# Sums, turns and products set in another order at the first items and at the end of column one

## The chip, the cores and the metric

The kernel runs on one core of one Trainium2 chip. The metric is the time of one execution on the device in microseconds (us), as the median of several runs. Three runs of the kernel before took 1510.43, 1511.97 and 1513.06 us.

## The reference

```
a, b: 4096 x 4096, float32; bias: 4096, float32
reference(a, b, bias) = tanh(a @ b + bias)
```

The output is 4096 x 4096 in float32. The kernel multiplies in fp16 and sums in fp32.

## The kernel before, in words

**Blocks.** The 4096 rows of a are 16 pairs of 2 x 128 rows; the 4096 columns of b are four column groups of 1024, called columns 0 to 3. For one pair and one column group the result has four blocks of 128 x 512. They are made with seven products instead of eight (a Strassen scheme in Winograd's form). The left operands are the four quarters a11, a12, a21, a22 of the pair's rows, turned so that the contraction lies on the partitions (128 x 2048 in fp16), and sums of them: s2 = a21 - a22, s5 = a12 - a11, s1 = a22 - a11, s6 = s2 + s1, s7 = s1 - s5. The right operands are b11 and b22 and the sums d1, d3, d4, e6, e7 of b's quarters, which stay in SBUF for a whole column. The products are m2 (s2, b11), m5 (s5, b22), m3 (a11, d3), m1 (s1, d1), m4 (a22, d4), m6 (s6, e6) and m7 (s7, e7). Each is 16 matmuls of 128 x 128 by 128 x 512 into one PSUM bank.

**Read-outs.** After a product, `after` (for the first three items `lead_after`) emits the steps that read its bank. After m2 VectorE adds the bias to bank z into bank d and subtracts it into s (first items: the bias minus z into bank c); after m5 it writes c = z - s; after m1 it writes cs - z; after m7 it writes o = ds - z. m3, m4 and m6 are read by ScalarE. m5, m1 and m7 accumulate in z, so each waits until the one before it has been read; m3 accumulates in c.

**Items and slots.** The unit of work is an item, a pair (or half the contraction of two pairs) in one column, numbered 0 to 60. Items 0 to 12 are column 0 and 13 to 28 column 1. Seven slots belong to each item: item n has the slots from 7n on, its products stand at fixed positions from there (`PRODUCTS`: m2 at 0, m5 at 2, m3 at 4, m1 at 5, m4 at 6, m6 at 8, m7 at 10), so m6 and m7 of an item lie among the products of the next. For items 0 to 2 (`LEAD` = 3) `FIRST` gives another assignment: m4, m2, m3, m1, m5, m6, m7. At each slot the work put down for it by `at_slot` is emitted first, in the order of registration, and then the product with its read-outs. Every engine runs its own instructions in the order in which they were emitted, so this order, written by hand, is the schedule.

**Natural items.** Items 0 to 12 and 26 to 28 load a from HBM as float32, cast by the DMA to fp16, with `load_nat` (lines 228, 237, 245) on POOL's queue; r = 1 brings the rows of a21 and a22, r = 0 those of a11 and a12, u = 0 and 1 the two halves of each. `turn` then lets VectorE transpose them (line 265), two halves for each quarter. `prepare` puts the turns and sums on slots. Turned quarters that later items use again are stored to DRAM by `keep` on SP's queue; other items fetch them from there by `fetch`.

**Column one's long stretch.** Items 17 to 24 run in pairs through `four`, which applies the scheme a second time (matmuls 256 wide). For it some right operands give up room: quarters of b11 and e6 and one quarter (T3) of d3, d4, b22 and e7 are held in DRAM and brought back at its end. `give_back`, called as `step(k)` from the last call of `four`, emits what the table `BACK` gives for step k: `bring_block` and `move` for the operands, `fetch` for the quarters a21 and a12 of item 25 (guests), `load_nat` for item 26. `move` uses POOL's queue at steps below 12 and SP's from there on. Behind this stretch come items 25 to 28, the end of column one; 27 and 28 each take half the contraction of two pairs and lead over to column two.

**The main loop** goes over the slots and, in each, over `PRODUCTS`; with the positions before, at most one product falls on a slot.

All VectorE sums have line 151 (`tt`), products outside `four` line 473, those inside 765 and 829.

Of the kernel before, what the change touches and what calls it, by code (L numbers as in the profile page):

```python
# [35 lines left out]
PRODUCTS = {  # L36
    0: ("m2", "s2", "b11"),
    2: ("m5", "s5", "b22"),
    4: ("m3", "a11", "d3"),
    5: ("m1", "s1", "d1"),  # L40
    6: ("m4", "a22", "d4"),
    8: ("m6", "s6", "e6"),
    10: ("m7", "s7", "e7"),
}
SLOTS = 7

LEAD = 3
FIRST = {0: 6, 2: 0, 4: 4, 5: 5, 6: 2, 8: 8, 10: 10}  # L50

LAST = (ds(0, 384), ds(384, 128))
# [38 lines left out]

BACK = {
    1: {
        ("e6", 0): 6, ("e6", 1): 7, ("m7", "t3"): 7, ("b11", 0): 10, ("b11", 1): 10, ("b11", 2): 10, ("b11", 3): 10,
        ("m5", "t3"): 10, ("m3", "t3"): 10,
        ("guest", "a21"): 8, ("guest", "a12"): 10, ("nat", 1): 11, ("m4", "t3"): 11,
    },
# [23 lines left out]
def kernel(  # L121
# [61 lines left out]
    partner, begins, ends_with, firsts = {}, {}, {}, {}  # L183
# [10 lines left out]
    twos = {*partner, *second}  # L194
    fours = {n for c in FOURS for n in range(begins[c], ends_with[c])}
    guests = {(ends_with[1], "a12"), (ends_with[1], "a21")}

    def beginning(n):
        return begins.get(items[n][0], len(items))

    def again(n):
        return items[n][3]

# [12 lines left out]

    nat, aset = {}, {}

    def load_nat(n, r):


        c, pairs, part, _ = items[n]
        for u in range(2):
            if n < LEAD:
                tl = wide.tile([P, 4, KQ // 2], fp16, name="nat", tag="wide")
                for q in (0, 2, 1, 3):
                    src = a[ds((2 * pairs[0] + r) * P, P), ds(q * KQ + u * KQ // 2, KQ // 2)]
                    nc.gpsimd.dma_start(  # L228
                        out=tl[ds(q * QP, QP), :, :],
                        in_=src.rearrange("(mb p) k -> p mb k", p=QP),  # L230
                    )
            elif part is None:
                pool, tag = (quads, ("a21", "a12")[u]) if n - 2 in fours and not r else (wide, "wide")
                tl = pool.tile([P, 2, KQ], fp16, name="nat", tag=tag)
                for q in (0, 2, 1, 3):
                    src = a[ds((2 * pairs[0] + r) * P + u * 2 * QP, 2 * QP), ds(q * KQ, KQ)]
                    nc.gpsimd.dma_start(  # L237
                        out=tl[ds(q * QP, QP), :, :],
                        in_=src.rearrange("(mb p) k -> p mb k", p=QP),
                    )  # L240
            else:
                tl = wide.tile([P, 4, KQ // 2], fp16, name="nat", tag="wide")
                for q in (0, 2, 1, 3):
                    src = a[ds((2 * pairs[u] + r) * P, P), ds(q * KQ + part * KQ // 2, KQ // 2)]
                    nc.gpsimd.dma_start(
                        out=tl[ds(q * QP, QP), :, :],
                        in_=src.rearrange("(mb p) k -> p mb k", p=QP),
                    )
            nat[n, r, u] = tl
# [55 lines left out]
    turns = [0]  # L305
# [547 lines left out]
    def give_back(c, step):  # L853
        for (name, part), at in BACK[c].items():
            if at == step:
                if name == "nat":
                    load_nat(ends_with[c] + 1, part)
                elif name == "guest":
                    fetch(ends_with[c], part)
                elif name in TWO:  # L860
                    move(name, c, False, part, queue=nc.gpsimd if step < 12 else nc.sync)
                elif name in ("b12", "b21"):
                    load_raw(name, c + 1, part, nc.sync)
                else:
                    bring_block(name, part)
# [441 lines left out]
    def prepare(n):  # L1307

        s0 = SLOTS * (n - 1)
        part = items[n][2]  # L1310
        if again(n):
            at_slot(s0, lambda: aset[n].update((i, aset[n - 2][i]) for i in QUADS))
        elif natural(n):
            loads = {0: (-5, -4), 1: (4, 5), 2: (6, 7)}.get(n, (s0 - 7, s0 - 4))
            for r in (1, 0):
                at_slot(loads[1 - r], load_nat, n, r)
                if n == 1 and r:
                    at_slot(loads[0], store_ends, "A")
            turns = {
# [4 lines left out]
            }.get(n, [(i, (s0 + x, s0 + y)) for i, (x, y) in {  # L1324
                "a22": (0, 0), "a21": (2, 2), "a11": (3, 4), "a12": (5, 5)
            }.items()])
            if n - 2 in fours:
                turns = [("a22", (3, 3)), ("a21", (4, 4)), ("a11", (5, 5)), ("a12", (6, 6))]
                turns = [(i, (s0 + x, s0 + y)) for i, (x, y) in turns]
            for name, at in turns:  # L1330
                at_slot(at[0], turn, n, name, 0)
            for name, at in turns:
                at_slot(at[1], turn, n, name, 1)
                if n == 0 and name == "a22":
                    at_slot(-1, asum, n, "s2", 0)
                if name in ("a11", "a22") and not stays(n):
                    at_slot({0: {'a22': -1, 'a11': 5}, 1: {'a22': 12, 'a11': 15}, 2: {'a22': 17, 'a11': 18}}.get(n, {}).get(name, at[1]), keep, n, name)
        else:
            behind = n - 2 in partner
            for name, at in (  # L1340
                ("a22", 1 if behind else 0), ("a21", 1),
                ("a11", -1 if n in second else 0 if behind else 2), ("a12", 4),
            ):
                if part == 1 and n - 2 in fours and name != "a12":
                    continue
                if name == "a12" and n - 2 not in twos and n > LEAD + 1 and n - 2 not in fours:
                    early_fetch.add(n)
                elif name != "a12" or n - 2 not in twos:
                    at_slot(s0 + at, fetch, n, name)
        late = stays(n)  # L1350
        end_ = n == len(items) - 1
        sums_at = {"s2": 4, "s5": 6, "s1": 9}
        sums_at["s6"] = 12 if late else 13 if end_ else 10
        sums_at["s7"] = 15 if late else 12 if end_ else 13
        if n == 0:
            at_slot(-1, asum, n, "s2", 1)
            at_slot(-1, keep, n, "a21")
            sums_at = {"s1": 10, "s5": 11, "s6": 12, "s7": 14}
        elif n == 1:
            sums_at = {"s2": 6, "s1": 9, "s5": 9, "s6": 13, "s7": 15}  # L1360
        elif n == 2:
            sums_at = {"s2": 6, "s1": 8, "s5": 9, "s6": 12, "s7": 14}
        elif n == 3:
            sums_at["s2"] = 3
        elif n - 2 in partner:
            sums_at["s2"] = 3
        if natural(n) and n - 2 in fours:
            sums_at["s2"], sums_at["s5"] = 5, 7
        if n - 2 in twos and n not in twos and part is None:
            sums_at["s5"] = 8  # L1370
        for name, at in sums_at.items():
            at_slot(s0 + at, asum, n, name)
            if natural(n) and name in ("s2", "s5") and not stays(n):
                at_slot(s0 + at, keep, n, "a21" if name == "s2" else "a12")
        if natural(n) and stays(n):
            for at, name in zip(LATER[part], ("a22", "a21", "a11", "a12")):
                at_slot(SLOTS * (n + 2) + at, keep, n, name)
        if n < LEAD:
            at_slot(s0 + 11, lead_add, n)
            if n:  # L1380
                at_slot(s0 + 4, lead_bias, n)
# [255 lines left out]
    for c in range(1, NC):  # L1637
        n = next(n for n in range(len(items)) if items[n][0] == c)
# [33 lines left out]
    for n in partner:  # L1672
        s0 = SLOTS * n
# [15 lines left out]
    for slot in range(1 - len(ORDER), SLOTS * len(items)):  # L1689
# [11 lines left out]
        elif slot == 3:  # L1701
            last_visit(0)
            last_visit(1)
        for pos, p in PRODUCTS.items():
            n, r = divmod(slot - pos, SLOTS)
            if r == 0 and n >= 0 and n not in fours:
                if n < LEAD:
                    product(n, *PRODUCTS[FIRST[pos]])
                elif p[0] not in ("m3", "m4") or n not in twos:
                    product(n, *p)  # L1710
        for group in groups.get(slot, ()):
            twice_four(*group)
# [30 lines left out]
```

## Time and profile before

| | |
|---|---|
| median of three runs | 1511.97 us (1510.43 to 1513.06) |
| the profiled execution's own time | 1510.32 us |
| its span, first to last instruction | 1508.6 us |
| mean granted TensorE clock | 0.999 |
| TensorE busy | 1495.9 us (99%) |
| VectorE busy | 1214.4 us (80%) |
| ScalarE busy | 402.9 us (27%) |
| POOL busy | 528.4 us (35%) |

The profile is one execution, and its times count from the first instruction. PE is TensorE, PEld its weight load, DVE is VectorE, ACT is ScalarE, SP issues DMAs only. A row of a timeline has its start, its duration, engine, line, operation, the tiles written and read, the shape and the number of instructions merged into it; a bracket has the idle time of the engine before the row and what ended it. Matmuls overlap, and their ends are modelled, so a row of 16 is drawn a little longer than the distance to the next. Rows of the windows' view have, for each engine, busy time and instructions, and at the end the granted clock, the DMA engines' busy share and GB/s. In the view of waits the three figures are the sum in us, the number and the longest.

### The profile page before, as it was taken

The page shows a single profiled execution, that of the slowest core. Times are in us where ns is not written, and L with a number is a line of the kernel's source. Part 1 is how long each engine was busy: PE and PEld are TensorE (multiplying, and loading weights), DVE is VectorE, ACT ScalarE, POOL GpSimd, SP SyncE. Part 2 cuts the span into 40 slices and gives each one's busy share as a digit, 9 for nine tenths or more (in the row PEclk, how much of TensorE's full clock was granted, in tenths as well). Part 3 has the DMA queues.
Part 4 walks back from the last instruction along what each step waited for, and adds up shares of the span by engine and source line. Part 5 has one row for each costly group of instructions (what it writes and reads, how often), then busy time and mean ns, then how long its engine had stood idle before and what let it go on. Part 6 is the DMA issues. An engine that isn't in the chain of part 4 may idle for free.

```text
span 1508.6 us, 24955 instructions
## 1 busy us (share of the span) xinstructions
PE 1495.9 (99%) x9461; PEld 925.3 (61%) x9461; DVE 1214.4 (80%) x1718; ACT 402.9 (27%) x909; POOL 528.4 (35%) x925
## 2 busy tenths in 40 slices
PE   9999999999999999998999999999999999999999
PEld 4444444444445788863444578888744458888887
DVE  6788977778787888967788788888758869888888
ACT  4431111111222233321123223333212222333332
POOL 8765454434523111255660321111434121111112
PEclk9999999999999999999999999999999999999999
DMA  9999999999999799899999988998899687888895
GB/s 183 178 243 265 294 265 258 226 220 178 183 345 308 259 324 344 309 317 255 186 265 324 276 267 317 335 342 303 307 304 225 201 277 274 303 312 305 321 345 190
DMA packets 209020, 412.47 MB, mean 273 GB/s; under 512 B 26114, under 2 KB 100354, under 8 KB 208900
## 3 DMA queue, kind: packets, MB, share of 16 engines
q0 software_dynamic: 124992, 220.00, 59.6%
q1 hardware_dynamic: 83236, 190.49, 35.6%
q8 instruction: 74, 1.21, 0.3%
q10 hardware_dynamic: 672, 0.39, 0.1%
q14 instruction: 46, 0.38, 0.1%
HBM read 351.80 MB, written 138.41 MB: 325 GB/s over the span
## 4 chain that ended last, share of the span: by engine, by line
PE 90%; DMA 6%; POOL 1%; issue 1%; DVE 1%; ACT 0%; POOLq 0%; DVEq 0%
PE ps L473 41%; PE ps L765 37%; PE ps L829 7%; PE ps L1419 5%; DMA nat<-in_a_dram 4%; DMA d<-away_m_t 1%; DMA out_dram<-o 1%; DMA e<-form_m 0%; DVE a L265 0%; DMA side<-in_b_dram 0%; POOL nat L228 0%; POOL nat L237 0%; POOL out_dram L1557 0%; ACT o L1552 0%; DVE a L151 0%
## 5 line engine op out<-in xcount | busy, mean ns | idle before, releaser
L473 PEld LDWEIGHTS <-a 128*128 128x128 f16 x2592 | 253.9, 98 | 312.2 <-issue 9.9
L765 PEld LDWEIGHTS <-h 128*128 128x128 f16 x2944 | 288.0, 98 | 35.8
L701 POOL DMA_DIRECT2D form<-form_m x196 | 103.9, 530 | 538.0 <-PE ps L765 484.8
L765 PEld LDWEIGHTS <-a 128*128 128x128 f16 x2208 | 216.0, 98 | 34.0 <-issue 0.9
L473 PE MATMUL ps<-b,a 128*128 128x512 f16 x868 | 200.0, 381 | 4.2 <-DVE s L151 4.2
L473 PE MATMUL ps<-d,a 128*128 128x512 f16 x800 | 180.8, 379 | 2.2 <-DVE ps L151 2.2
L265 DVE STREAM_TRANSPOSE a<-nat 128x1024 f16<-128x1024 f16 (+3 forms) x178 | 155.9, 918 | 23.0 <-PE ps L473 13.1
L473 PE MATMUL ps<-e,a 128*128 128x512 f16 x700 | 159.2, 379 | 0.0
L151 DVE TENSOR_TENSOR a<-a,a 128x2048 f16<-128x2048 f16 (+1 forms) x123 | 148.0, 1203 | 0.2
L765 PE MATMUL ps<-form,h 128*128 128x256 f16 x1136 | 144.8, 273 | 0.0
L375 POOL DMA_DIRECT2D b<-in_b_dram x208 | 112.0, 546 | 87.7 <-PE ps L473 32.0
L151 DVE TENSOR_TENSOR h<-a,h 128x1024 f16<-128x1024 f16 x184 | 124.8, 685 | 16.6 <-PE ps L765 16.5
L473 PEld LDWEIGHTS <-s 128*128 128x128 f16 x688 | 67.3, 98 | 79.9
L473 PE MATMUL ps<-d,s 128*128 128x512 f16 x496 | 112.1, 379 | 0.0
L765 PE MATMUL ps<-form,a 128*128 128x256 f16 x896 | 111.5, 273 | 0.2
L829 PE MATMUL ps<-d,a 128*128 128x512 f16 x480 | 108.2, 379 | 0.0
L237 POOL DMA_DIRECT2D nat<-in_a_dram x144 | 76.4, 541 | 76.6 <-DMA nat<-in_a_dram 35.0
L851 ACT CAST ps<-zeros 128x256 f32<-128x256 f16 x192 | 68.8, 380 | 128.6 <-DVE s L151 69.0
L829 PEld LDWEIGHTS <-a 128*128 128x128 f16 x608 | 59.5, 98 | 65.9
L151 DVE TENSOR_TENSOR ds<-ds,ps 128x512 f32<-128x512 f32 (+1 forms) x126 | 83.3, 672 | 9.2 <-PE ps L829 8.3
L151 DVE TENSOR_TENSOR ps<-ps,x 128x256 f32<-128x256 f32 x96 | 41.2, 429 | 47.3 <-PE ps L765 37.6
L498 ACT ACTIVATE o<-ps 128x512 f32<-128x512 f32 x78 | 46.9, 601 | 117.4 <-issue 69.8
(167 smaller groups left out, 1971.3 us busy)
## 6 DMA issues: line engine op xcount, KB each, us to landing
form<-form_m POOLq DMA_DIRECT2D x196, 512.0 KB, 7.3
a<-scratch SPq DMA_DIRECT2D x148, 512.0 KB, 7.5
out_dram<-o SPq DMA_DIRECT2D x186, 256.0 KB, 6.1
nat<-in_a_dram POOLq DMA_DIRECT2D x256, 128.0 KB, 6.9
scratch<-a SPq DMA_DIRECT2D x48, 512.0 KB, 7.2
b<-in_b_dram POOLq DMA_DIRECT2D x176, 128.0 KB, 5.6
form_m<-stage POOLq DMA_DIRECT2D x18, 512.0 KB, 6.0
scratch<-a SPq DMA_DIRECT2D x32, 256.0 KB, 7.7
```

What stands on the lines that cost most here:

```text
L151: nc.vector.tensor_tensor(out=out_, in0=in0, in1=in1, op=op)
L237: nc.gpsimd.dma_start(out=tl[ds(q * QP, QP), :, :], in_=src.rearrange("(mb p) k -> p mb k", p=QP),)
L265: nc.vector.transpose(dst[:, ds(b0 * tb, n * tb), :].rearrange("P (b t) (mb p) -> P mb b t p", t=tb, p=QP), src[:, :, ds(b0, n), :].rearra ...
L375: nc.gpsimd.dma_start(out=dst[ds(q * QP, QP), ds(t, nt)], in_=src)
L473: nc.tensor.matmul(st[where], at, bt, start=(what == "m2" or n < LEAD and what == "m1") and i == 0, stop=i == len(ts_) - 1, skip_group_che ...
L498: nc.scalar.activation(o, src, TANH)
L701: nc.gpsimd.dma_start(out=rights[what, name], in_=forms[what, name])
L765: nc.tensor.matmul(to, at, bt, start=False, stop=t == TP - 1, skip_group_check=True)
L829: nc.tensor.matmul(to[:, half], at[:, t // TB, t % TB], bop[right, t // TB][:, t % TB, half], start=anew and t == 0, stop=t == T - 1, skip ...
L851: nc.scalar.copy(bank(n, 0, where)[:, HALF[half]], zeros)
L1419: nc.tensor.matmul(mb[m % 4, j], aq[m, kt // T][:, kt % T, :], right(kt, j), start=fresh and kt == k0, stop=stop and kt == k1 - 1, skip_gr ...
```

## The change

It moves work among slots and queues; the arithmetic stays.

- Item 1: s1 and s5 go from slot 9 to 10, item 2: s5 from 16 to 17, so behind the read-out of their own item's m2. Item 4: the turns of a22 go from slot 21 to 22, behind the read-outs of item 3's m2.
- Item 26: the second halves of a11 and a12 are turned at slot 183 instead of 180 and 181, and s5 goes from 182 to 183; m2 of item 26 is at 182. Item 27: a22 is turned at 183 and 184 instead of 182. The two keeps of a11 and of s5 go with them.
- m7 of item 25 is put at position 9 instead of 10, which is slot 184, where it is emitted ahead of m5 of item 26. m4 of item 26 is put at position 3 instead of 6, ahead of m3.
- The end of the long stretch: the T3 quarter of d3 goes from step 10 to step 11, behind the loads of item 26's r = 1 rows; that of d4 from step 11 to step 14, which is on SP's queue. The fetch of the guest a12 is emitted ahead of b11 (another queue).

```diff
+BEHIND = {"m7": 9}, {"m4": 3}
...
 BACK = {
     1: {
-        ("e6", 0): 6, ("e6", 1): 7, ("m7", "t3"): 7, ("b11", 0): 10, ("b11", 1): 10, ("b11", 2): 10, ("b11", 3): 10,
-        ("m5", "t3"): 10, ("m3", "t3"): 10,
-        ("guest", "a21"): 8, ("guest", "a12"): 10, ("nat", 1): 11, ("m4", "t3"): 11,
+        ("e6", 0): 6, ("e6", 1): 7, ("m7", "t3"): 7, ("guest", "a21"): 8, ("guest", "a12"): 10,
+        ("b11", 0): 10, ("b11", 1): 10, ("b11", 2): 10, ("b11", 3): 10,
+        ("m5", "t3"): 10, ("nat", 0): 11, ("nat", 1): 11, ("m3", "t3"): 11, ("m4", "t3"): 14,
     },
...
+    def order_of(n):
+        if n < LEAD:
+            return [(pos, PRODUCTS[FIRST[pos]]) for pos in PRODUCTS]
+        moved = {ends_with[1]: BEHIND[0], ends_with[1] + 1: BEHIND[1]}.get(n, {})
+        return sorted((moved.get(p[0], pos), p) for pos, p in PRODUCTS.items())
...
-    def load_nat(n, r):
+    def load_nat(n, r, parts=(0, 1)):
         c, pairs, part, _ = items[n]
-        for u in range(2):
+        for u in parts:
...
                 if name == "nat":
-                    load_nat(ends_with[c] + 1, part)
+                    load_nat(ends_with[c] + 1, 1, (part,))
...
+            if n == 4:
+                turns[0] = "a22", (s0 + 1, s0 + 1)
+            if n - 3 in fours and part is not None:
+                turns[0] = "a22", (s0 + 1, s0 + 2)
             if n - 2 in fours:
-                turns = [("a22", (3, 3)), ("a21", (4, 4)), ("a11", (5, 5)), ("a12", (6, 6))]
+                turns = [("a22", (3, 3)), ("a21", (4, 4)), ("a11", (5, 8)), ("a12", (6, 8))]
...
         elif n == 1:
-            sums_at = {"s2": 6, "s1": 9, "s5": 9, "s6": 13, "s7": 15}
+            sums_at = {"s2": 6, "s1": 10, "s5": 10, "s6": 13, "s7": 15}
         elif n == 2:
-            sums_at = {"s2": 6, "s1": 8, "s5": 9, "s6": 12, "s7": 14}
+            sums_at = {"s2": 6, "s1": 8, "s5": 10, "s6": 12, "s7": 14}
...
         if natural(n) and n - 2 in fours:
-            sums_at["s2"], sums_at["s5"] = 5, 7
+            sums_at["s2"], sums_at["s5"] = 5, 8
...
-        for pos, p in PRODUCTS.items():
-            n, r = divmod(slot - pos, SLOTS)
-            if r == 0 and n >= 0 and n not in fours:
-                if n < LEAD:
-                    product(n, *PRODUCTS[FIRST[pos]])
-                elif p[0] not in ("m3", "m4") or n not in twos:
+        for n in (slot // SLOTS - 1, slot // SLOTS):
+            if n < 0 or n in fours:
+                continue
+            for pos, p in order_of(n):
+                if SLOTS * n + pos == slot and (p[0] not in ("m3", "m4") or n not in twos):
                     product(n, *p)
```

## The prediction

> **What bounds the kernel now.** I read the busy shares first, then the waits of TensorE, its timeline around each wait, and last the timelines of the engines and queues that end those waits.
>
> ```profile
> PE 1495.9 (99%) x9461; PEld 925.3 (61%) x9461; DVE 1214.4 (80%) x1718; ACT 402.9 (27%) x909; POOL 528.4 (35%) x925
> ```
>
> TensorE is busy for 1495.9 of 1508.6 us, so only its own gaps can be won. The view of waits, for TensorE alone, names those inside the kernel:
>
> ```profile
> PE ps L473 <- DVE s L151: 4.2, 2, 3.5
> PE ps L473 <- DVE ps L151: 2.2, 2, 1.8
> PE ps L473 <- DVE a L151: 0.4, 1, 0.4
> ```
>
> Five waits, all on VectorE (DVE). The timeline of TensorE places them; the bracket is the idle time before the row.
>
> ```profile
> 120.51 3.62 PE L473 MATMUL ps<-e,a 128*128 128x512 f16 x16
> 125.94 3.61 PE L473 MATMUL ps<-d,a 128*128 128x512 f16 x16 [1.82 <-DVE ps L151]
> ...
> 150.61 3.61 PE L473 MATMUL ps<-d,a 128*128 128x512 f16 x16 [0.34 <-DVE ps L151]
> ...
> 168.73 3.61 PE L473 MATMUL ps<-b,a 128*128 128x512 f16 x16 [0.69 <-DVE s L151]
> ...
> 699.75 1.04 PE L473 MATMUL ps<-side,a 128*128 128x512 f16 x4 [0.42 <-DVE a L151]
> ...
> 710.33 5.30 PE L473 MATMUL ps<-b,a 128*128 128x512 f16 x16 [3.50 <-DVE s L151]
> ```
>
> From the chain of waits, two long pieces with no gap follow the two groups, and one transfer precedes them:
>
> ```profile
> 139.17 8.35 DMA nat<-in_a_dram
> ...
> 168.73 293.69 PE ps L473 x1360
> ...
> 710.33 126.17 PE ps L473 x576
> ```
>
> A product of 16 matmuls thus takes 16 x 293.69 / 1360 = 3.455 us. The product of 120.51 should be followed at 123.97 and was followed at 125.94: 1.97 lost, 0.15 more than its bracket (the drawn end of a matmul overlaps the next start). So the losses are 1.97, 0.50, 0.85, 0.58 and 3.66. The row at 710.33 lasts 5.30 instead of 3.62, 1.68 more, and the stretch shows why:
>
> ```profile
> 709.90:713.40 3.50, 3.07 (x9) 1.18 (x9) 3.50 (x6) 0.00 (x0) 1.33 (x3) 0.62 1.16 256
> ```
>
> The granted clock (third figure from the end) was 0.62 after the idle time of 3.50; after the one of 1.82 the product took its usual 3.61. [...]
>
> All the losses together are 1.97 + 0.50 + 0.85 + 0.58 + 3.66 + 1.68 = 9.24 us, the most that the change can win.
>
> **Part one, the first items (3.3 us of loss).** VectorE's timeline ahead of the three waits:
>
> ```profile
> 120.67 2.37 DVE L265 STREAM_TRANSPOSE a<-nat 128x1024 f16<-128x1024 f16 x2 [2.22 <-DMA nat<-in_a_dram]
> 122.97 1.18 DVE L151 TENSOR_TENSOR s<-a,a 128x2048 f16<-128x2048 f16 x1
> 124.07 1.21 DVE L151 TENSOR_TENSOR a<-a,a 128x2048 f16<-128x2048 f16 x1
> 125.20 0.69 DVE L151 TENSOR_TENSOR ps<-bias_bc,ps 128x512 f32<-128x512 f32 x1
> ...
> 147.60 1.25 DVE L265 STREAM_TRANSPOSE a<-nat 128x1024 f16<-128x1024 f16 x1 [1.74 <-DMA nat<-in_a_dram]
> 148.77 1.18 DVE L151 TENSOR_TENSOR a<-a,a 128x2048 f16<-128x2048 f16 x1
> 149.87 0.69 DVE L151 TENSOR_TENSOR ps<-bias_bc,ps 128x512 f32<-128x512 f32 x1
> ...
> 165.15 2.36 DVE L265 STREAM_TRANSPOSE a<-nat 128x1024 f16<-128x1024 f16 x2
> ```
>
> Item 1: its s1 and s5 (122.97, 124.07) stand ahead of m2's read-out (125.20), for which m3 waits. Put behind, the read-out runs at 122.97 and ends at 123.66, before m3 is due at 123.97: the 1.97 go. The sums then run where they end no later than now plus one read-out, about 125.9; m1, the first user of s1, is due at 127.4 and m5 at 130.9. Nothing else on VectorE moves.
>
> Item 2: only s5 (148.77) moves. The turn at 147.60 stays ahead of the read-out, and it waits for a transfer issued at 139.17 that lands 8.35 later, at 147.5. TensorE being early does not hurry that transfer. The read-out runs 148.77 to 149.46, so m3 starts at 149.50 instead of 150.61. It is due at 150.11 - 1.97 = 148.14, so 1.36 is lost anew: of the first 2.47 us, 1.11 remains.
>
> Item 3: m5 is due five products after 149.50, at 166.78. The two turns of 165.15 (item 4's a22) go one slot back, behind m2's two read-outs, which then run 165.15 to 166.5 and are in time. So 168.73 becomes 166.78. Item 4's a22 is then turned by 168.9; its first user, the sum s2, stands two slots after the turn's new one.
>
> Part one gives 1.95 us. From there the gapless piece of 293.69 only moves; VectorE has no new work.
>
> **Part two, behind column one (5.9 us of loss).** Times are those of before, without the shift. VectorE and TensorE:
>
> ```profile
> 697.28 1.30 DVE L265 STREAM_TRANSPOSE a<-nat 128x256 f16<-128x256 f16 x2 [1.74 <-DMA nat<-in_a_dram]
> 698.51 1.18 DVE L151 TENSOR_TENSOR a<-a,a 128x2048 f16<-128x2048 f16 x1
> ...
> 704.88 1.24 DVE L265 STREAM_TRANSPOSE a<-nat 128x1024 f16<-128x1024 f16 x1
> 707.86 1.25 DVE L265 STREAM_TRANSPOSE a<-nat 128x1024 f16<-128x1024 f16 x1 [1.73 <-DMA nat<-in_a_dram]
> ...
> 709.60 0.67 DVE L151 TENSOR_TENSOR s<-ps,bias_bc 128x512 f32<-128x512 f32 x1
> ...
> 711.33 2.48 DVE L265 STREAM_TRANSPOSE a<-nat 128x512 f16<-128x512 f16 x4
> ```
>
> ```profile
> 688.81 3.62 PE L473 MATMUL ps<-d,a 128*128 128x512 f16 x16
> ...
> 729.28 1.03 PE L473 MATMUL ps<-side,a 128*128 128x512 f16 x4
> ```
>
> 688.81 is item 25's m3, and m1 and m4 follow. The second half of item 26's a11 goes behind m2's read-outs, so s2 (698.51) starts near 695.5, when VectorE now begins its wait, and ends at 696.7: m2 of item 26 is on time at 699.17. It ends at 702.6; m6 and now m7 of item 25 fill TensorE to 709.54, when m5 is due. VectorE meanwhile: read-outs to 704.1, the halves of a11 and a12 (1.30, 1.2) to 706.6, s5 (1.2) to 707.8. So m5 waits for nothing, 1.7 to spare: 0.58, 3.66 and 1.68 all go, 5.92 together.
>
> What takes their place must fit: item 27's a22 and a21 (1.24, then s1 with 1.2, 1.25, 2.48), m7's last step and m5's read-out (0.7 each) take VectorE to about 715. m3 right behind m5 would be due at 713.0 and wait 2; with m4 between them it is due at 716.45. At the end m2 of item 27 comes at 723.36 instead of 729.28. Its four read-outs stand behind m1's read-out, two sums (1.2 each) and two turns (2.4), the first two done by 729.9 against m5's 730.3: covered by 0.4, because m4 no longer lies between.
>
> **The T3 transfers.** POOL issues in order:
>
> ```profile
> 672.17 0.75 POOL L627 DMA_DIRECT2D d<-away_m_t  x1 [0.35 <-DMA b<-form_m]
> ...
> 675.51 1.16 POOL L237 DMA_DIRECT2D nat<-in_a_dram  x2 [1.12 <-DMA b<-form_m]
> ...
> 684.06 1.55 POOL L627 DMA_DIRECT2D d<-away_m_t  x2
> ...
> 691.73 0.53 POOL L237 DMA_DIRECT2D nat<-in_a_dram  x1 [0.58 <-DMA d<-away_m_t]
> ```
>
> ```profile
> 672.17 10.04 DMA d<-away_m_t
> ...
> 684.06 6.28 DMA d<-away_m_t
> ```
>
> At 672.17 m3's pair goes out, then eight loads for item 26, then at 684.06 m4's pair. m3's pair now goes behind the eight loads, and m4's to SP's queue, behind the fetch of a11 and ahead of m6's store. m4's is needed at 695.7: free, and the store behind it waits for ScalarE anyway. m3's first half is needed at 688.81, the second four matmuls later at 689.67. Early bound: the loads move up by 675.51 - 672.17 = 3.34, the pair goes out at 680.7, lands after 6.28 at 687.0, the second half about 1 later: no wait. Late bound: it lands as m4's pair does now, at 690.34 and 691.45 (the load of 691.73 waits for it, less an issue gap of 0.28): 1.78. I take 0.8, near the middle, since the same bytes are moved in either order but two issues fewer stand ahead.
>
> [...]
>
> **Sum.** 1.95 + 5.92 - 0.8 = 7.07 us. The profiled execution took 1510.32 (span 1508.6 and 1.7 around it) and would take 1503.2; it lies 1.65 below the median of the runs, 1511.97, from which I forecast 1504.9.
>
> **Rivals.** *T3 late.* POOL holds m3's pair behind loads that each wait for an earlier landing. For: latencies here reach 10.04. Issued at 684.06 with that latency, its halves land at 694.1 and about 694.9: idle 5.2, over the 3.50 that cost clock, so 1.7 more; of 7.87 us, 1 remains, 1511.0. At latency 8 it is 692.9 in the second half, idle 3.2, no clock lost: 4.7 remain, 1507.3. Against: 6.28 for the pair last issued there.
>
> *Slower.* The wait for item 27's tile is not removed but moved: it now stands ahead of m5's read-out, and m3 behind that. The tile landed just before 707.86; the new place is reached at 709.9, and m3 has 1.6 to spare, so it decides from a landing at 711.5 on, 1 us for each us, and 1.7 for the clock once idle passes 3.5. To end 3 us slower than before it must land near 720. For: SP's two keeps, now at one slot, compete. Against: they start after 705, and the landing would have to slip by 12.
>
> *No change:* the DMA paces the first items (the 1.74 and 2.22 waits) and the loads for 26 to 28, so that TensorE, sooner, waits elsewhere for the same landings. Against: behind 168.73 and 710.33 no row of TensorE waits for a DMA or VectorE. Time 1512. In a half form it gives back part one alone: 1506.9.
>
> *More:* no T3 wait and an earlier 147.5: up to 9.24, 1502.7.
>
> **Numbers.** Forecast 0.62 (1504.1 to 1505.9), T3 late 0.15, half form 0.06, more 0.06, no change 0.06, slower 0.05. A difference under 0.2% (3 us) can't be told from none. Faster: forecast, half form, more and most of T3 late, 0.84; same: no change and the rest of it, 0.11; slower 0.05. The range 1502.5 to 1510.0 leaves out the last two cases and the worst T3, and has a little for the spread of the runs.
>
> **What would show it.** Right: no TensorE wait near 124; one of about 0.2 to 1.2 near 149; none near 167; m5 of item 26 without a wait and no stretch with a clock below 1.00 after it; a DMA wait on d before item 25's m3 of 0 to 1.8. Wrong: a wait of m3 over 3 us, a VectorE wait at item 26's m3 or item 27's m5, or a new gap between 200 and 650.

## The result, and the profile after

| | before | after |
|---|---|---|
| median, same chip (6 runs each) | 1510.96 us (1508.90 to 1513.06) | 1503.53 us (1502.12 to 1505.88) |
| the profiled execution's own time | 1510.32 us | 1502.82 us |
| its span | 1508.6 us | 1501.1 us |
| mean granted TensorE clock | 0.999 | 1.0 |

The ratio of the times is 0.9954 (95% interval 0.9940 to 0.9967), a gain of about 7 us. Forecast were 1504.9 us, a gain of 7.07, and a range of 1502.5 to 1510.0. In the diff's new line numbers the sums have line 152, the turns 272, the products 480.

The busy shares of the page after, and the view of waits for TensorE; outside the warm-up only one wait on another engine is left:

```profile
PE 1494.3 (100%) x9461; PEld 925.3 (62%) x9461; DVE 1213.8 (81%) x1718; ACT 403.9 (27%) x909; POOL 527.0 (35%) x923
```

```profile
PE ps L480 <- DVE ps L152: 0.3, 1, 0.3
```

TensorE's timeline after, at the places shown of before (start, duration, operation; the bracket is the idle time ahead):

```profile
120.51 3.62 PE L480 MATMUL ps<-e,a 128*128 128x512 f16 x16
123.96 3.62 PE L480 MATMUL ps<-d,a 128*128 128x512 f16 x16
...
148.60 3.61 PE L480 MATMUL ps<-d,a 128*128 128x512 f16 x16 [0.30 <-DVE ps L152]
...
165.86 3.62 PE L480 MATMUL ps<-b,a 128*128 128x512 f16 x16
...
686.12 3.87 PE L480 MATMUL ps<-d,a 128*128 128x512 f16 x16
...
701.05 6.21 PE L480 MATMUL ps<-e,a 128*128 128x512 f16 x28
707.09 3.62 PE L480 MATMUL ps<-b,a 128*128 128x512 f16 x16
710.54 7.07 PE L480 MATMUL ps<-d,a 128*128 128x512 f16 x32
717.45 3.62 PE L480 MATMUL ps<-d,s 128*128 128x512 f16 x16
720.90 1.03 PE L480 MATMUL ps<-side,a 128*128 128x512 f16 x4
```

Item 1's m3 follows its predecessor after 3.45 us, so its wait is gone. Item 2's m3 starts 0.46 later than a product after 144.68 (start of the one ahead) would let it. Item 3's m5 has no bracket; it stands at 165.86 against 168.73, so TensorE is 2.87 us early. The row of 686.12, item 25's m3, is drawn with 3.87 instead of 3.62: 0.28 us are lost ahead of its first matmul and 0.26 ahead of its fifth, just behind the landings of its T3 pair at 685.98 and 687.20. Behind column one m6 and m7 of item 25 run as one row of 28 matmuls, m5 of item 26 follows at once, m4 and m3 make one row of 32. Item 27's m2 starts at 720.90 against 729.28, 8.38 us early. The clock was never reduced in between, as the windows' view shows (third figure from the end):

```profile
706.90:710.40 3.50, 3.50 (x18) 1.61 (x17) 3.50 (x6) 0.00 (x0) 1.91 (x4) 1.00 1.06 244
```

VectorE's timeline after, at the three places that the change reorders:

```profile
121.76 0.67 DVE L152 TENSOR_TENSOR ps<-bias_bc,ps 128x512 f32<-128x512 f32 x1
122.34 1.20 DVE L152 TENSOR_TENSOR s<-a,a 128x2048 f16<-128x2048 f16 x1
...
146.71 1.25 DVE L272 STREAM_TRANSPOSE a<-nat 128x1024 f16<-128x1024 f16 x1 [2.17 <-DMA nat<-in_a_dram]
147.88 0.67 DVE L152 TENSOR_TENSOR ps<-bias_bc,ps 128x512 f32<-128x512 f32 x1
...
701.00 0.68 DVE L152 TENSOR_TENSOR s<-ps,bias_bc 128x512 f32<-128x512 f32 x1
701.59 2.42 DVE L272 STREAM_TRANSPOSE a<-nat 128x256 f16<-128x256 f16 x3
704.05 1.23 DVE L152 TENSOR_TENSOR a<-a,a 128x2048 f16<-128x2048 f16 x1
...
711.55 0.69 DVE L152 TENSOR_TENSOR ps<-ps,s 128x512 f32<-128x512 f32 x1
```

At 121.76 the read-out is ahead of s1. At 147.88 the read-out still stands behind a turn that waited 2.17 us for its tile. At 701.59 come the three halves, then s5 (704.05), which ends at 705.28, 1.8 ahead of m5 of item 26 at 707.09. m5's read-out ends at 712.24; m3 needs it at 714.0.

**The end of the span holds a loss that no view of waits names.** The last product, before and after, from TensorE's timelines:

```profile
1503.33 1.91 PE L765 MATMUL ps<-form,a 128*128 128x256 f16 x16
```

```profile
1494.73 1.91 PE L772 MATMUL ps<-form,a 128*128 128x256 f16 x16
```

TensorE ends 8.60 us earlier, but the span is only 7.5 shorter: 5.3 us follow 1503.33 before, 6.4 follow 1494.73 after. The final stores are not the reason, since the last one lands 1.82 after its issue before and 1.80 after. The trace's records of the sequencers, which the timeline leaves out, show it in the DRAIN instructions ahead of the joint end of all engines:

```
                           start     end       length
POOL, closing DRAIN before 1500.81   1505.90   5.09
POOL, closing DRAIN after  1492.21   1500.32   8.11
SP, DRAIN before           1507.83   1507.84
SP, DRAIN after            1499.09   1499.10
```

Before, POOL had drained 1.9 us ahead of SP; after, the joint end waits 1.2 us for POOL.

### The profile page after: what moved, and what is told of

Read it like the earlier page. It is cut to its first block, busy times and chain, and to the rows that moved or that the text cites. A ratio compares the mean times of both kernels' runs of the same rounds, so it can differ in the third digit from the quotient of the medians.

```text
span 1501.1 us, 24949 instructions
## 1 busy us (share of the span) xinstructions
PE 1494.3 (100%) x9461; PEld 925.3 (62%) x9461; DVE 1213.8 (81%) x1718; ACT 403.9 (27%) x909; POOL 527.0 (35%) x923
## 4 chain that ended last, share of the span: by engine, by line
PE 88%; DMA 7%; POOL 2%; DVE 1%; issue 1%; ACT 0%; POOLq 0%; DVEq 0%
PE ps L480 43%; PE ps L772 37%; PE ps L836 7%; DMA nat<-in_a_dram 3%; DMA b<-in_b_dram 2%; POOL b L382 1%; DMA land<-in_a_dram 1%; DMA b<-away_m_t 1%; POOL land L1471 1%; DMA e<-form_m 0%; POOL nat L235 0%; DMA d<-away_m_t 0%; DVE a L272 0%; POOL side L1519 0%; DVE e L152 0%
```

## The experiments

Theory: each removed wait is worth what TensorE lost at it, and the three late edits (turns behind the read-outs, m7 first, m4 first) are needed together. Rivals: the DMA paces both places and TensorE would find the same waits later; the T3 moves cost or bring something of their own.

### One part at a time

**e1: the first items alone**, on the kernel before.

```diff
+            if n == 4:
+                turns[0] = "a22", (s0 + 1, s0 + 1)
-            sums_at = {"s2": 6, "s1": 9, "s5": 9, "s6": 13, "s7": 15}
+            sums_at = {"s2": 6, "s1": 10, "s5": 10, "s6": 13, "s7": 15}
-            sums_at = {"s2": 6, "s1": 8, "s5": 9, "s6": 12, "s7": 14}
+            sums_at = {"s2": 6, "s1": 8, "s5": 10, "s6": 12, "s7": 14}
```

> Part one alone (items 1, 2 and 4), all else as before. The prediction's theory: the order of VectorE's steps costs the three early waits; the kernel is 1.95 us faster (ratio 0.9987) if item 3's tile lands at 147.5 as it did in the profile of before, up to 2.9 us (0.9981) if it lands near 146.7 as in the changed kernel, and the wait left at item 2's m3 follows that landing one to one. Behind column one everything stays: waits of 0.42 and 3.50 and a clock below 1.00. Rival (the DMA paces the first items): less than 0.5 us faster, with new waits of TensorE between 168 and 460.

Measured: 1508.06 us against 1510.22, ratio 0.9982 (0.9973 to 0.9990), by which it gains 2.7 us. The waits at items 1 and 3 are gone and item 2's m3 lost 1.92 in this profile. TensorE's timeline of e1 behind column one keeps both old waits:

```profile
699.69 1.04 PE L473 MATMUL ps<-side,a 128*128 128x512 f16 x4 [1.94 <-DVE a L151]
...
709.52 2.81 PE L473 MATMUL ps<-b,a 128*128 128x512 f16 x9 [2.75 <-DVE s L151]
```

So part one is a gain by itself, and the later waits stay when TensorE comes early: from start to start they lose 2.10 and 2.92 here, against 0.58 and 3.66 before. In before VectorE had stood 1.74 and 1.73 us for tiles ahead of the two.

**e2: the order behind column one alone** (the table entries of T3 and the first items as before).

```diff
+BEHIND = {"m7": 9}, {"m4": 3}
...
-        ("m5", "t3"): 10, ("nat", 0): 11, ("nat", 1): 11, ("m3", "t3"): 11, ("m4", "t3"): 14,
+        ("m5", "t3"): 10, ("m3", "t3"): 10, ("nat", 0): 11, ("nat", 1): 11, ("m4", "t3"): 11,
...
+            if n - 3 in fours and part is not None:
+                turns[0] = "a22", (s0 + 1, s0 + 2)
-                turns = [("a22", (3, 3)), ("a21", (4, 4)), ("a11", (5, 5)), ("a12", (6, 6))]
+                turns = [("a22", (3, 3)), ("a21", (4, 4)), ("a11", (5, 8)), ("a12", (6, 8))]
-            sums_at["s2"], sums_at["s5"] = 5, 7
+            sums_at["s2"], sums_at["s5"] = 5, 8
```

> The order of turns, sums and products behind column one alone; the first items and the T3 transfers as before. The prediction's theory: 5.92 us faster (ratio 0.9961), the three early waits of before stay, item 25's m3 waits for no DMA, m5 of item 26 waits for nothing and the clock stays at 1.00. Rival (the T3 and load moves are what lets the tiles come in time): a wait of over 1 us at item 26's m2, m5 or m3, and less than 4.5 us.

Measured: 1504.38 us, ratio 0.9959 (0.9947 to 0.9972), by which it gains 6.2 us. m2, m5 and m3 of item 26 have no wait, the clock stays at 1.00. By the ratios the two parts add to 8.9 us, and the whole change gains 7.0. The 1.9 us between them are less than the three intervals together; if they are real, the T3 moves or a later wait take them back.

The waits at the first items, which e2 keeps, are there but of other sizes: 0.43, 1.29 and 0.87 lost at items 1, 2 and 3, against 1.97, 0.50 and 0.85 in the profile before.

### The T3 transfers

**e3: both T3 quarters at their old places.**

```diff
-        ("m5", "t3"): 10, ("nat", 0): 11, ("nat", 1): 11, ("m3", "t3"): 11, ("m4", "t3"): 14,
+        ("m5", "t3"): 10, ("m3", "t3"): 10, ("nat", 0): 11, ("nat", 1): 11, ("m4", "t3"): 11,
```

> The changed kernel with both T3 transfers at their places of before (m3's at step 10 ahead of the loads of item 26, m4's at step 11 on POOL's queue). If the move only cost, as the prediction has it: the two small DMA waits of the changed kernel at item 25's m3 (0.28 and 0.26 lost) are gone and nothing else is late, so about 0.5 us faster than the changed kernel, ratio to before 0.995. Rival (the move pays, by bringing item 26's tiles sooner): a wait at item 26's m2 of over 0.3 us and a time equal to or above the changed kernel's.

Measured: 1502.89 us, ratio 0.9945 (0.9933 to 0.9958). Item 25's m3 waits for nothing. But the profile has a wait that the prediction does not name. TensorE's and VectorE's timelines of e3 at item 28:

```profile
760.45 3.61 PE L480 MATMUL ps<-d,a 128*128 128x512 f16 x16 [0.99 <-DVE ps L152]
```

```profile
754.93 1.23 DVE L152 TENSOR_TENSOR d<-b,b 128x2048 f16<-128x2048 f16 x1 [3.31 <-DMA b<-in_b_dram]
756.08 1.22 DVE L152 TENSOR_TENSOR s<-a,a 128x2048 f16<-128x2048 f16 x1
757.21 1.22 DVE L152 TENSOR_TENSOR side<-side,b 128x2048 f16<-128x2048 f16 x1
758.56 1.23 DVE L152 TENSOR_TENSOR d<-b,b 128x2048 f16<-128x2048 f16 x1
759.70 0.69 DVE L152 TENSOR_TENSOR ps<-ps,s 128x512 f32<-128x512 f32 x1
```

VectorE waits 3.31 us for a block of b for column two, and m5's read-out (759.70), for which m3 of item 28 waits, stands behind the sums. After, the same sum was held up for less and the read-out was in time:

```profile
755.63 1.23 DVE L152 TENSOR_TENSOR d<-b,b 128x2048 f16<-128x2048 f16 x1 [1.00 <-DMA b<-in_b_dram]
```

TensorE's loss there, from start to start, was 0 after and in a_again, e5, e6, e7 and e12, 0.03 in e11, 0.47 in e4, 0.61 in e2, 0.93 in e8, 1.16 in e3 and 1.73 in e9. It is the next wait in line: a landing that TensorE, now earlier, sometimes meets.

**e4: m4's T3 on POOL, behind m3's.**

```diff
-        ("m5", "t3"): 10, ("nat", 0): 11, ("nat", 1): 11, ("m3", "t3"): 11, ("m4", "t3"): 14,
+        ("m5", "t3"): 10, ("nat", 0): 11, ("nat", 1): 11, ("m3", "t3"): 11, ("m4", "t3"): 11,
```

> The changed kernel with m4's T3 pair on POOL's queue at step 11, right behind m3's, in place of SP's queue. Theory of the shared engines: without m4's pair beside it POOL's queue is faster by about a microsecond there, m3's pair lands before it is needed and item 25's m3 waits under 0.1 us. Theory of the place alone: m3's pair still stands behind eight loads, lands as in the changed kernel, and the wait stays at 0.4 to 0.7 us. Both: the stores behind the fetch of item 25's a11 on SP's queue land in 7 to 10 us again, where the changed kernel had 16 to 20.

Measured: 1503.29 us, ratio 0.9950 (0.9937 to 0.9964). No wait at item 25's m3: its pair, issued at 679.70, landed at 685.84 and 686.74. SP's stores, which had taken 16 to 20 us, took 6 to 8 again. The pair on SP's queue was thus the reason of those.

**a_again: the changed kernel once more**, unchanged, to see which of its waits recur.

> The changed kernel once more, on this chip, for its spread. If the two small waits at item 25's m3 are a race of two transfers against TensorE that five of six profiles with m4's pair on SP's queue or behind m3's have won, this profile shows between 0 and 0.6 us there; if they come with the change, again about 0.5. The wait at item 2's m3 should again be the landing of item 3's tile, 0.1 to 1.9 us. Ratio to before 0.9955.

Measured: 1503.64 us, ratio 0.9956 (0.9944 to 0.9969). Item 25's m3 did not wait this time (after: 0.28 and 0.26 in its two halves), and item 2's m3 lost 1.18 instead of 0.46. Both are races with a landing; whether m4's pair on SP makes m3's later is not settled, since a_again, e5, e6, e7 and e8 have it there and show no wait either.

**The end.** By POOL's closing DRAIN the 14 profiles fall into two groups; no run was made to test why.

| | POOL issues | POOL's closing DRAIN | last matmul's start to the end of the span |
|---|---|---|---|
| before, e1, e2, e3, e4, e9 | 916 | 5.09 us | 3.64 to 3.65 us |
| after, a_again, e5, e6, e7, e8, e11, e12 | 914 | 8.11 to 8.12 us | 4.74 to 4.76 us |

The second group is that of m4's T3 on SP. So the move goes with 1.1 us at the end of the program, 800 us behind its place, in every profile. e3 and e4 are without it, and their ratios lie lower, though their intervals overlap with those of after and a_again. e1 and e2 are without it too: of the 1.9 us that they have together over the whole change, 1.1 are found here and up to 0.5 at item 25's m3. What it is that lengthens the drain, the number of POOL's issues or something else of the move, was not tried.

### Behind column one, one edit undone at a time

**e5: the products in their old order.**

```diff
-BEHIND = {"m7": 9}, {"m4": 3}
+BEHIND = {}, {}
```

> The changed kernel with m7 of item 25 and m4 of item 26 at their old positions (m5 of item 26 right behind m6, m3 right behind m1's slot order of before). Theory of the prediction: m5 then comes due one product sooner, 3.45 us, against 1.7 to spare, so it waits about 1.7 for s5 (703.64 due, s5 done at 705.28 in the changed kernel's profile); m7 and then m3 wait for nothing, because m7 now lies between m5 and m3. 1.7 us slower than the changed kernel, clock stays at 1.00. Rival (the moved turns and sums are the whole gain, the products' order is idle): no wait at item 26's m5 and the changed kernel's time.

**e6: m4 alone at its old place.**

```diff
-BEHIND = {"m7": 9}, {"m4": 3}
+BEHIND = {"m7": 9}, {}
```

> The changed kernel with only m4 of item 26 at its old position, m7 of item 25 stays ahead of m5. Theory: m3 comes due right behind m5 (710.54 in the changed kernel's profile) and waits for m5's read-out, which ended at 712.24: a wait of 1.7 us at m3, nothing else, and 1.7 us slower than the changed kernel. Rival: m5's read-out comes sooner once m4 is gone, no wait, same time.

Measured: e5 1504.80 us against 1509.71, ratio 0.9963 (0.9952 to 0.9974); e6 1504.50, ratio 0.9963 (0.9951 to 0.9975). TensorE's timeline of e5, then TensorE's and VectorE's of e6:

```profile
705.15 3.63 PE L480 MATMUL ps<-b,a 128*128 128x512 f16 x16 [1.53 <-DVE a L152]
```

```profile
711.28 3.63 PE L480 MATMUL ps<-d,a 128*128 128x512 f16 x16 [1.60 <-ACT o L579]
```

```profile
710.53 0.69 DVE L152 TENSOR_TENSOR ps<-ps,s 128x512 f32<-128x512 f32 x1
```

From start to start 1.69 us are lost at m5 in e5, and 1.76 at m3 in e6. The wait that m7 covers comes back at m5; with m7 first but m4 last it moves on to m3. In e6 the profile names ScalarE as the releaser, but m5's read-out on VectorE ended at 711.22, just ahead of the start at 711.28, and that is the wait which the order makes. With the turns and sums moved, the two moves together are worth about 1.7, and m7 first without m4 first nothing: it only carries the wait from m5 to m3. This rests on the traces: the intervals of the times overlap with those of after and a_again. m4 first alone was not tried.

**e7: item 27's a22 turned ahead of the read-outs again.**

```diff
-            if n - 3 in fours and part is not None:
-                turns[0] = "a22", (s0 + 1, s0 + 2)
```

> The changed kernel with item 27's a22 turned at slot 182 again, ahead of item 26's m2 read-outs. Theory: the second half waits for item 27's tile (landed at 703.7 in the changed kernel), the read-outs end near 706.2, the halves of a11 and a12 and s5 come behind them until 709.8, and m5 of item 26, due at 707.1, waits 2.7 us; under the idle time of 3.5 that cost clock, so the clock stays at 1.00: 2.7 us slower than the changed kernel. Rival (m7's place alone covers the tile): a wait under 0.5 us.

Measured: 1506.46 us, ratio 0.9980 (0.9970 to 0.9991). VectorE's, TensorE's timelines and the windows of e7:

```profile
702.10 1.25 DVE L272 STREAM_TRANSPOSE a<-nat 128x1024 f16<-128x1024 f16 x1 [4.33 <-DMA nat<-in_a_dram]
704.49 1.25 DVE L272 STREAM_TRANSPOSE a<-nat 128x1024 f16<-128x1024 f16 x1 [1.14 <-DMA nat<-in_a_dram]
705.66 0.67 DVE L152 TENSOR_TENSOR ps<-ps,bias_bc 128x512 f32<-128x512 f32 x1
```

```profile
710.56 5.31 PE L480 MATMUL ps<-b,a 128*128 128x512 f16 x16 [2.64 <-DVE a L152]
```

```profile
710.50:714.00 3.50, 3.44 (x11) 1.42 (x12) 3.50 (x7) 0.00 (x0) 2.01 (x5) 0.66 0.84 171
```

VectorE stands 4.33 and 1.14 us at the two turns for their tiles, and m2's read-out comes only at 705.66. m5 loses 2.80, even with m7 as cover, and the clock fell: the product took 5.31 instead of 3.62. Of its ten timed runs the five with a mean clock of 0.999 took 1508.1 us in the mean, the five with 1.000 took 1505.8. Taken back alone, this turn costs the most of the late edits.

**e8: item 26's halves and s5 at their old slots.**

```diff
-                turns = [("a22", (3, 3)), ("a21", (4, 4)), ("a11", (5, 8)), ("a12", (6, 8))]
+                turns = [("a22", (3, 3)), ("a21", (4, 4)), ("a11", (5, 5)), ("a12", (6, 6))]
-            sums_at["s2"], sums_at["s5"] = 5, 8
+            sums_at["s2"], sums_at["s5"] = 5, 7
```

> The changed kernel with the second halves of item 26's a11 and a12 and s5 at their old slots 180, 181 and 182, ahead of m2's read-outs. Theory: s2 stands again behind a11's second half, whose tile landed at 694.4, so it ends near 696.9 where m2 is due at 696.7: a wait of 0.2 (0 to 1) us at m2; the read-outs start as soon as m2 ends and m5, behind m7, waits for nothing. So 0.2 us slower than the changed kernel, which no time can show: this edit was worth the 0.58 of before and no more. Rival (the halves' place is what frees the read-outs): a wait of over 1 us at m5.

Measured: 1503.06 us, ratio 0.9952 (0.9935 to 0.9970). At the place of the edit only m2 of item 26 waits, and loses 0.33 from start to start, so the gain does not hang on this edit once the others are in:

```profile
697.09 1.04 PE L480 MATMUL ps<-side,a 128*128 128x512 f16 x4 [0.17 <-DVE a L152]
```

**e9: m7 first as the only edit**, on the kernel before.

```diff
+BEHIND = {"m7": 9}, {}
```

> The kernel before with one edit: m7 of item 25 put ahead of m5 of item 26; turns, sums, T3 transfers and m4 as before. Theory (a product moved into the gap is worth its 3.45 us and the clock on top): the wait at m2 of item 26 stays (0.6 to 2.1), m5 comes due one product later, just about when the read-outs end, and waits about 0.2; m3, right behind m5, waits about 1.3 for m5's read-out, which stands behind item 27's a21; the clock stays at 1.00. So 3.7 us faster than before (ratio 0.9975). Rival (VectorE's order is what has to change): m5 still waits over 2 us and the clock falls.

Measured: 1507.39 us against 1509.73, ratio 0.9986 (0.9978 to 0.9995), by which it gains 2.1 us and not the expected 3.7. TensorE's timeline of e9 shows what took the rest:

```profile
714.47 3.63 PE L480 MATMUL ps<-d,a 128*128 128x512 f16 x16 [0.79 <-DVE ps L152]
...
764.55 3.61 PE L480 MATMUL ps<-d,a 128*128 128x512 f16 x16 [1.56 <-DVE ps L152]
```

m5 of item 26 no longer waits; m2 loses 0.80, as expected, m3 0.96 behind it and item 28's m3 1.73, the unforeseen one that e3 has too. The clock stayed at 1.00. At item 26 itself m7 alone thus takes the loss from 5.92 to 1.76 in this profile, so the late edits overlap, and what each is worth depends on which others are in.

### Two attempts to go further

**e11: the second half of item 3's a22 turned two slots later**, so that item 2's read-out need not wait for its tile (the 2.17 of 146.71).

```diff
-                3: (("a22", (15, 15)), ("a21", (17, 17)), ("a11", (18, 18)), ("a12", (19, 19))),
+                3: (("a22", (15, 17)), ("a21", (17, 17)), ("a11", (18, 18)), ("a12", (19, 19))),
```

> The changed kernel with the second half of item 3's a22 turned at slot 17 instead of 15, so behind the read-out of item 2's m2 and not ahead of it. Theory: the wait left at item 2's m3 (0.07 to 1.9 us in the profiles with the change of part one) is that turn's wait for its tile and goes altogether; item 3's m5 is then due near 165.4, where its read-outs end, and waits at most 0.3. So the first stretch gains 3.0 to 3.3 us in all, 0.3 to 0.9 more than the changed kernel in most runs (ratio 0.995). Rival (the DMA paces these items): the wait comes back at item 3's m2 or m5 with the same size.

Measured: 1505.04 us, ratio 0.9967 (0.9954 to 0.9979), not better. TensorE's, then VectorE's timeline of e11:

```profile
148.22 3.62 PE L480 MATMUL ps<-d,a 128*128 128x512 f16 x16
...
162.82 1.02 PE L480 MATMUL ps<-side,a 128*128 128x512 f16 x4 [0.62 <-DVE ps L152]
...
167.46 3.61 PE L480 MATMUL ps<-b,a 128*128 128x512 f16 x16 [1.03 <-DVE s L152]
...
689.63 3.86 PE L480 MATMUL ps<-d,a 128*128 128x512 f16 x16 [1.58 <-DMA d<-away_m_t]
```

```profile
157.48 1.30 DVE L272 STREAM_TRANSPOSE a<-nat 128x256 f16<-128x256 f16 x2 [3.49 <-DMA nat<-in_a_dram]
```

The wait of item 2's m3 is gone, but VectorE now stands 3.49 us at the next tile, and item 3's m2 and m5 lose 0.78 and 1.20. Here the DMA does pace the items: this edit only moved the wait. The T3 wait was 1.75 and 0.25 in this profile, the most of any run.

**e12: e11, and the second block of column two's d3 one slot later**, so that item 28's read-out is not behind it.

```diff
-            at_slot(s1 + 8, bsum, "d3", blk)
+            at_slot(s1 + 8 + (c == 2 and not part and i), bsum, "d3", blk)
```

> The kernel of the run before this one, and at the change to column two the second block of d3 is summed one slot later, behind m5's read-outs of item 28. Theory: the wait at item 28's m3 (0.5 to 1.2 us in four profiles, 0 in the others), in which VectorE stood at that sum for the transfer of column two's b, is gone or under 0.3; together with the edit at item 3 this version is 0.5 to 1.5 us faster than the changed kernel, ratio 0.9945. Rival: the first block's sum, one slot ahead, holds the read-outs as long, and nothing changes.

Measured: 1505.70 us, ratio 0.9965 (0.9951 to 0.9978). Item 28's m3 does not wait, as in about half of the runs without this edit; item 3's m5 loses 1.19 again, and item 2's m3 0.36, behind an earlier tile for which VectorE stood 3.94 us at 141.37. Between 974 and 984 us, in column two, the profiles of e12 and e6 also lose 1.3 and 1.4 us after VectorE stood 2.60 and 2.73 for an output store; no other profile has this, and none of the edits reaches that place. No version here is measurably faster than the changed kernel.

## Why the prediction was right, and where it was not

In the profiled executions, as TensorE's advance over before:

| step | predicted | measured |
|---|---|---|
| part one | 1.95 | 2.87 |
| part two | 5.92 | 5.94 (8.38 at 720.90, less 2.87 and the step at 574, plus the T3 wait) |
| T3, at item 25's m3 | -0.8 | -0.53 |
| end of the program | not foreseen | -1.11 |
| small steps at 574 and 1414 us | not foreseen | 0.10 and 0.23 |
| sum | 7.07 | 7.50 |

**Part one: right mechanism, one term mis-sized.** "TensorE being early does not hurry that transfer" put item 3's tile at 147.5 as before and left 1.36 at item 2's m3. The turn started at 146.71 and 0.46 was lost. The step that was mis-sized is this landing, and it is no constant: over the profiles with part one that keep the turn there the loss runs from 0.07 (e6) to 1.92 (e1), with a mean of 0.91 over nine. The forecast took one draw of a landing that varies by nearly 2 us. The loss that part one removes is a draw too: e2 and e9, with the old order of the first items, lost 0.43 and 0.18 at item 1, 1.29 and 1.31 at item 2, 0.87 and 0.86 at item 3. From the product of 120.51 to item 3's m5 the three profiles with the old order take 47.64 us in the mean and the nine 45.80. That is 1.84 us, near the 1.95 forecast; the 2.87 of the one pair is in part luck. Items 1 and 3 came out as worked; the turns of item 4 behind the read-outs caused no wait.

**Part two: right in each step.** m2 of item 26 on time, m6 and m7 as cover, m5 with 1.8 to spare (1.7 predicted), no clock loss. e5, e6 and e8 gave back 1.7, 1.8 and 0.3 where their expectations, worked out from the changed kernel's profile, have 1.7, 1.7 and 0.2. With m3 right behind m5 it was to "wait 2": e6 has 1.76. Item 27's read-outs, "covered by 0.4", caused no gap either. The *slower* rival, that the wait for item 27's tile only moves, did not occur: m3 stood 1.8 behind the end of m5's read-out. e7 shows what that tile costs where it stands first, 2.80 and the clock. Expected there was a full clock: the 3.50 us of idle ahead of the one fall in before had been taken as the bound for a fall, which was the author's estimate and wrong, since e7's clock fell behind 2.64. The *T3 late* rival's "idle 3.2, no clock lost" rests on the same estimate. Nor is the 1.68 for the clock a part of every run of before: of its 49 timed runs beside the experiments 20 have a mean clock of 1.000, while the profile of before, with one fall of 3.413 us to half speed, has 0.999.

**T3: right at its place, wrong in "free".** 0.53 lies inside the bounds of 0 and 1.78 and near the 0.8 taken; but the other profiles have 0 (six of them), 0.54 (e12) and 2.0 (e11), so the late bound was a little short. That m4's pair on SP's queue slows m3's on POOL's, the first theory of e4, was not shown: over the eight profiles with m4's pair on SP the first half of m3's took 5.94 to 6.67 us, and 6.14 in e4 without it. What was slow was SP's side. m4's pair was issued at 665.81 and 666.29 and landed 16.83 and 21.62 us later, against 6.28 and 6.61 on POOL before, and the stores behind it took 19.55, 17.92 and 16.26. The pair was still 5 us ahead of m4 at 693.28, so this cost nothing there. "m4's is needed at 695.7: free" failed elsewhere: the same move goes with 1.1 more at the end, at POOL's closing drain. The working followed the queue that gets the transfers and not the one that loses them.

**"No change", in a small form.** The DMA does pace both places a little: at item 2 (VectorE stood 2.17 us for the tile after, and 3.49 at the next one in e11, whose order only moved the wait) and at item 28 (3.31 us for a block of b in e3), where "no row of TensorE waits" in before but up to 1.73 is lost once TensorE comes earlier. The prediction looked for the next late wait only as far as item 27.

The forecast of 1504.9 against 1503.53 is thus near, with two misses of opposite sign that cancel in part: the early landing (0.9 better, in this pair of profiles) and the drain (1.1 worse). It started from a median of 1511.97 over three runs; from the 1510.96 over six, the same gain leads to 1503.9. The rest is within the spread of the runs.

## What to carry to other kernels

Cost a wait by the distance of the starts, put a read-out ahead of whatever stands for a transfer, and look one wait further: a product moved ahead as cover can be worth nothing where the next one's read-out is not covered too (e6), and most of the loss where another order stands behind it (e9). A transfer moved to another queue is priced on both queues, up to the last instruction of the program: compare the end of the last matmul with the end of the span. And a wait for a landing is a range, not a number (0.07 to 1.92 us at item 2's m3 here); one profile of it is a single draw.

## What was not expected of the hardware

**The clock fell after shorter idle times than the 3.50 us of before.** In before the records of the clock show TensorE at half clock for 3.413 us from 710.75 on, 0.42 behind the start of the product ahead of which it had been idle for 3.50. The clock also fell behind drawn idle times of 2.75 in e1 (granted 0.61 over 710.0 to 713.5, with 1.00 over the 3 us ahead) and of 2.64 in e7 (0.66 over 710.5 to 714.0, likewise 1.00 over the 3.5 us ahead). It stayed at full clock behind 1.82 (before), 1.94 (e1), 1.60 (e6) and 1.53 (e5): the rows that follow have their usual lengths, 3.61 to 3.63 for 16 matmuls and 1.04 for the four in e1. So the idle time at which the clock falls lies between 1.94 and 2.64 us, an estimate from these seven drawn waits alone. Where it lies between them, and whether the length of the idle time alone decides, was not shown. The stretches of full clock that the traces of before and after record last 706.559, 795.305 and 1495.038 us: 207, 233 and 438 times the 3.4133 of the fall.

**One transfer, two queues.** The same T3 pair took 6.3 and 6.6 us on POOL's queue and 16.8 and 21.6 on SP's, where the stores behind it took 16 to 20 us. The trace's packets show how the pair goes: as 128 of 4096 bytes on POOL's queue, as 1024 of 512 bytes on SP's (the pages count 1024 more packets under 2 KB after than before, and 128 fewer of 2 to 8 KB). The small pieces alone did not make it slow: at the end of column two four transfers of the same size into d go on SP's queue in 512-byte packets too, and land 3.69 to 5.79 us after their issue. The view of the DMAs after, at the pair on SP (665.8 to 687.9) and at those four (1087.6 to 1097.8); q0 is POOL's queue with packets, MB and the share of 16 engines, and the last figure of the other rows is the median us to landing:

```profile
q0 software_dynamic: 1678, 4.10, 69.0%
...
d<-away_m_t SPq DMA_DIRECT2D x2, 256.0 KB, 19.2
```

```profile
q0 software_dynamic: 26, 0.10, 2.9%
...
d<-away_m_t SPq DMA_DIRECT2D x4, 256.0 KB, 4.7
```

So the slow transfers went in 512-byte packets while POOL's queue took 69.0% of the engines, the quick ones in the same packets while it took 2.9%. Whether the size of the packets matters beside a busy POOL queue was not tried by itself.

**A drain with two lengths.** POOL's closing drain took 5.09 or 8.11 us in 14 profiles, nothing between, in step with 916 or 914 transfers that POOL had issued. What makes it longer is open.
